# Output gates by seven block products for two pairs of chunks, in a bidirectional hybrid encoder layer

## The chip, the cores and the metric

The kernel runs on one core of a Trainium2 chip. The metric is the device time of one execution in microseconds. The kernel before takes 1054.59 us (median of 3 runs, 1054.48 to 1054.64).

## The reference, cut to what matters

One layer over 1024 tokens of width 1024, all in float32:

```python
h  = rmsnorm(x)
gb, gc, gv, q, k, v, go, lr_f, lr_b = split_cols(h @ w_in)    # go: 512 columns
y_a = gb * dwconv3(gc * gv, conv_a)
y_b = silu(go) * headnorm(gla(q, k, v, decay(lr_f)) + flipped gla(..., decay(lr_b)))   # 4 heads
x  = x + rmsnorm(concat(y_a, y_b) @ w_out)
h  = rmsnorm(x)
u  = dwconv3(h @ w_up)                                        # 2 x 2816 columns
x  = x + rmsnorm((silu(u_gate) * u_val) @ w_down)
```

The change is about `go`, the output gates: `h @ w_in[:, 2560:3072]`, then silu. Each head of the gated linear attention (gla) has 128 of these columns.

## The kernel before

**Arithmetic.** TensorE multiplies in a reduced float format, so each operand is split in a high and a low part: ACT casts the high part (`copy`), DVE subtracts it from the original (`tensor_sub`) and gets the low part, and a product takes three passes (high x high, high x low, low x high). A weight chunk of 128 columns by 1024 tokens, `feature_chunk` (matmuls at L257), is 8 blocks of the contraction x 3 passes x 2 halves of the tokens = 48 matmuls of 128x512. `load_cols` loads its weights (DMA at L224) and splits them (L215 on ACT, L216 on DVE).

**Stages, in the order of TensorE.** (1) Norm, transposes into `hT` (the high and low parts of h, transposed, in two halves of 512 tokens) and the projection for v and the two small decay inputs, one tile of 128 tokens after another. (2) Four output gate chunks, `swish_gate(h)`: 48 matmuls into a PSUM tile `pgo`, then silu on ACT into `yT[4 + h]` (L298). (3) Four heads, `gla_head(h)`, interleaved with 12 chunks of the short convolution (`conv_tile`, chunks `gc`, `gv`, `gb`). (4) The product with w_out and the second norm. (5) The up projection, whose products are made with block sums: a 2 x 2 block product in 7 products instead of 8, 12 matmuls each (`product`, called under L859). (6) The down projection, seven `big_product`s of 132 matmuls (L1190), which run in the order 2, 1, 3, 6, 5, 7, 4. (7) The last norm and the output.

**One head.** On TensorE: `pqk` (queries and keys, a feature chunk), `pg` (L513, log decay), `pko` (L547, transposes of the decayed keys `cum`), `kv` (L580, states), `sc` (L561, scores), `po` (L635 scores x values, L638 queries x states). Between them, in TensorE's queue, stand the matmuls of convolution chunks and of the next head's `pqk`. On the way from `pg` to `pko`: ACT Abs, Exp, Ln of `pg` into `cum`; DVE subtracts (L521), runs two scans (L522, L523), copies `cl` (L527, L528); ACT Exp; DVE multiplies queries and keys (L536, L534, L537) and ends with `cum` times keys (L538). From `kv` to L638: ACT copies the states from PSUM into `S` (L588, L592), DVE runs 28 dependent steps over `S` (L597, L601). In DVE's queue the operations of head h and of head h + 1 are mixed.

**Jobs on GpSimd (POOL).** The up and down projections need sums of blocks of their weights. A job loads two tiles of 512 KB, makes four 128x512 sums or differences (`block_sums` at L108 to L111, `down_end` at L146 to L149), and stores the tiles to DRAM. There are 17 jobs: wu0 to wu3 (w_up), wp4 and wp5 (w_up, chunks 4 and 5), q0 to q10 (w_down). `side()` takes the next job from the list; with `ahead=1` its loads are begun one job before its sums. Before the change `side` is called in token tiles 2 to 7, after each gate chunk and at the first head, so twelve jobs (wu0 to wu3, q0 to q7) are begun there; five follow in the w_out stage. `tc.issue_after(i)` holds an instruction behind another one of the same engine, in that engine's queue.

Of the kernel before, what the change touches and what calls it, by code (L numbers as in the profile page):

```python
# [40 lines left out]
def kernel(  # L41
# [114 lines left out]
    jobs = [(up_begin, up_end, i) for i in range(4)] + [(down_begin, down_end, q) for q in range(8)]  # L156
    jobs += [(pair_begin, pair_end, c) for c in (4, 5)] + [(down_begin, down_end, q) for q in range(8, NQ)]
# [136 lines left out]
    def swish_gate(h):
        w = load_cols([(w_in, O_GO + h * P, P)], f"go{h}")
        ps = feature_chunk(w, hT, f"pgo{h}")
        yT[4 + h] = ypool.tile([P, L], F32, tag="y", name=f"yT{4 + h}")
        nc.scalar.activation(yT[4 + h], ps, AF.Silu)  # L298

    act_table("natural_log_exp_and_others")  # L300
    with ExitStack() as n1:
# [195 lines left out]
    left = []  # L497

    def gla_head(h):

# [43 lines left out]
        def decayed():  # L544
# [4 lines left out]
            nc.scalar.copy(tiles["koT"], pk)  # L549
# [179 lines left out]

# [595 lines left out]
```

## Time and profile before

| | |
|---|---|
| median of the runs | 1054.59 us |
| the profiled execution, its own time | 1054.48 us |
| its span | 1052.8 us (1.7 us lie around it) |
| granted TensorE clock, mean | 0.998 |
| busy: PE, PEld, DVE, ACT, POOL | 1040.6, 871.0, 797.7, 466.5, 260.4 us |
| stage: token tiles | until 66 us |
| stage: gates | 66 to 111 us, then `pqk` of head 0 until 122 us |
| stage: four heads and the convolution | 122 to 321 us |
| stage: w_out | 321 to 436 us |
| stage: up | 436 to 836 us |
| stage: down | 836 to 1016 us, and the tail to 1052.8 us |

PE is TensorE's matmuls, PEld its weight loads (they run beside matmuls), DVE VectorE, ACT ScalarE, POOL GpSimd, SP the engine that issues most DMAs. In the timeline a line gives start, duration, engine, line of the program, operation, and out<-in; a bracket at the end gives the idle time of the engine before it and what ended that. `x2` groups two instructions of one kind.

### The profile page before, as it was taken

Reading aid. Unit: us, or ns where it says so; the run is one execution under the profiler, and the core shown is the slowest. Engines: PE = TensorE matmul, PEld = TensorE weight load, DVE = VectorE, ACT = ScalarE, POOL = GpSimd, SP = SyncE. Lnnn points to the kernel's source line nnn. Section 1 sums busy time; section 2 is a strip of 40 time slices with the busy share of each in tenths; the row PEclk is TensorE's granted clock in tenths of the full one; section 3 lists DMA queues with packets and bytes.
Section 4 is the critical chain, followed back from the end, with each engine's and each line's share of the span. In section 5 each row is a group of like instructions: output and inputs, shape, how many; then the busy total and the mean of one; then the engine's idle time right before and its main releaser. Section 6 shows DMA issues by size and latency. Waiting matters only on the chain.

```text
span 1052.8 us, 14126 instructions
## 1 busy us (share of the span) xinstructions
PE 1040.6 (99%) x5409; PEld 871.0 (83%) x5409; DVE 797.7 (76%) x991; ACT 466.5 (44%) x637; POOL 260.4 (25%) x253
## 2 busy tenths in 40 slices
PE   8999999999999999999999999999999999999997
PEld 7998888888888888887888888888888888888886
DVE  6843379889877877989977977987897875545566
ACT  5431353553434345644434344344443564344443
POOL 2797830000015810002242241241240000000011
PEclk9999999999999999999999999999999999999999
DMA  8888730110166853264323233332323687666555
GB/s 287 283 272 289 249 110 21 52 49 21 40 222 207 290 181 110 90 180 140 121 90 110 100 103 98 124 112 85 110 100 121 200 275 258 206 197 197 167 170 209
DMA packets 125701, 164.48 MB, mean 156 GB/s; under 512 B 16177, under 2 KB 83138, under 8 KB 125634
## 3 DMA queue, kind: packets, MB, share of 16 engines
q1 hardware_dynamic: 113762, 121.24, 36.3%
q0 software_dynamic: 11152, 40.38, 10.8%
q10 hardware_dynamic: 720, 1.97, 0.5%
q8 instruction: 42, 0.69, 0.3%
q14 instruction: 25, 0.20, 0.1%
HBM read 117.16 MB, written 46.40 MB: 155 GB/s over the span
## 4 chain that ended last, share of the span: by engine, by line
PE 94%; DVE 4%; DMA 1%; issue 0%; ACT 0%; SPq 0%; DVEq 0%; ACTq 0%
PE pb L859 16%; PE pc L859 11%; PE pdb L1190 10%; PE pa L859 10%; PE pw L785 8%; PE pgv L257 4%; PE pgc L257 4%; PE pqk L257 4%; PE pgo L257 4%; PE pv L368 4%; PE pgb L257 3%; PE pdd L1190 3%; PE pdc L1190 3%; PE pda L1190 3%; PE pdl L1190 1%; PE kv L580 1%
## 5 line engine op out<-in xcount | busy, mean ns | idle before, releaser
L1190 PE MATMUL pdb<-d 128*128 128x512 f32 (+1 forms) x495 | 109.5, 382 | 0.0
L1190 PEld LDWEIGHTS pdb<-d 128*128 128x128 f32 x495 | 90.8, 188 | 18.0
L859 PE MATMUL pb<-t,uv 128*128 128x512 f32 x264 | 63.4, 389 | 0.0
L1238 POOL DMA_DIRECT2D x2r<-x2d x4 | 2.2, 542 | 227.9 <-DMA d_8r<-actd 218.6
L859 PEld LDWEIGHTS pb<-t,uv 128*128 128x128 f32 x264 | 49.6, 188 | 10.3
L1073 DVE TENSOR_TENSOR cg<-cv,pb 128x512 f32<-128x512 f32 x22 | 15.1, 685 | 35.2 <-PE pb L859 17.7
L1121 ACT ACTIVATE uu<-uu 128x1024 f32<-128x1024 f32 x22 | 23.4, 1062 | 36.1 <-DVE uu L1043 35.9
L123 POOL COPY wp4g<-ident 128x1 f32<-128x1 f32 x1 | 0.2, 191 | 154.6 <-PE pgc L257 154.6
L1079 ACT COPY cg<-pa 128x512 f32<-128x512 f32 x22 | 12.9, 585 | 46.5 <-PE pa L859 46.5
L1042 DVE SCALAR_TENSOR_TENSOR uv<-cv,prm,uv 128x1023 f32<-128x1023 f32 x22 | 31.7, 1439 | 0.0
L1190 PE MATMUL pdc<-d 128*128 128x512 f32 x132 | 30.1, 389 | 0.0
L1190 PE MATMUL pdd<-d 128*128 128x512 f32 x132 | 30.1, 389 | 0.0
L1190 PEld LDWEIGHTS pdd<-d 128*128 128x128 f32 x132 | 24.8, 188 | 5.1
L1190 PEld LDWEIGHTS pdc<-d 128*128 128x128 f32 x132 | 24.8, 188 | 5.1
L1043 DVE SCALAR_TENSOR_TENSOR uu<-cg,prm,uu 128x1023 f32<-128x1023 f32 x22 | 28.9, 1314 | 0.0
L1043 DVE SCALAR_TENSOR_TENSOR uv<-cv,prm,uv 128x1023 f32<-128x1023 f32 x22 | 28.1, 1277 | 0.0
L1042 DVE SCALAR_TENSOR_TENSOR uu<-cg,prm,uu 128x1023 f32<-128x1023 f32 x22 | 28.1, 1276 | 0.0
L929 POOL TENSOR_TENSOR us61r<-uv6r 128x512 f32<-128x512 f32 x1 | 1.3, 1343 | 106.4 <-ACT us4bh L731 106.4
L1124 DVE TENSOR_TENSOR uu<-uu,uv 128x1024 f32<-128x1024 f32 x22 | 27.3, 1240 | 0.0
L597 DVE SCALAR_TENSOR_TENSOR S<-S,dec 64x128 f32<-64x128 f32 x56 | 19.2, 344 | 10.3 <-ACT S L588 8.5
L1041 ACT ACTIVATE uu<-cg,prm 128x1024 f32<-128x1024 f32 x22 | 25.2, 1144 | 2.9 <-ACT uv L1041 1.5
L1041 ACT ACTIVATE uv<-cv,prm 128x1024 f32<-128x1024 f32 x22 | 25.4, 1155 | 1.2 <-DVE cv L1101 0.6
(1204 smaller groups left out, 3170.0 us busy)
## 6 DMA issues: line engine op xcount, KB each, us to landing
actd<-as SPq DMA_DIRECT2D x20, 512.0 KB
x<-in_x_dram SPq DMA_DIRECT2D x16, 512.0 KB, 6.0
actd<-uu SPq DMA_DIRECT2D x10, 512.0 KB, 3.5
x2d<-x SPq DMA_DIRECT2D x8, 512.0 KB, 3.3
actd<-uu SPq DMA_DIRECT2D x10, 256.0 KB, 2.0
out_dram<-o POOLq DMA_DIRECT2D x5, 512.0 KB, 6.6
x2r<-x2d POOLq DMA_DIRECT2D x4, 512.0 KB, 3.7
x2r<-x2d SPq DMA_DIRECT2D x4, 512.0 KB, 3.6
```

The source lines that it names most:

```text
L257: nc.tensor.matmul(o[hf], wt[:, k, :], act[hf][a][:, k, :], start=(k == 0 and wt is wh and a == 0), stop=(k == KT - 1 and wt is wl))
L368: keep(nc.tensor.matmul(ps[:, n * 512 : n * 512 + VH], a[:, k, sl], w[:, k % 2, n * VH : (n + 1) * VH], start=(j == 0), stop=(j == 3 * KT ...
L597: nc.vector.scalar_tensor_tensor(S[0:DK, c + 1, :], S[0:DK, c, :], dec[0:DK, c : c + 1], S[0:DK, c + 1, :], op0=ALU.mult, op1=ALU.add)
L785: ins = nc.tensor.matmul(ps[:, n * HALF : (n + 1) * HALF], a[:, k, sl], w[:, n * HALF : (n + 1) * HALF], start=(i == 0 and q == 0), stop=( ...
L859: nc.tensor.matmul(o, w[:, k, :], m[:, k, :], start=start and k == 0 and q == 0, stop=k == 3 and q == 2, skip_group_check=True)
L1041: nc.scalar.activation(u, src, AF.Copy, scale=ffn_tap(1, r))
L1042: nc.vector.scalar_tensor_tensor(u[:, 1:L], src[:, 0 : L - 1], ffn_tap(0, r), u[:, 1:L], op0=ALU.mult, op1=ALU.add)
L1043: nc.vector.scalar_tensor_tensor(u[:, 0 : L - 1], src[:, 1:L], ffn_tap(2, r), u[:, 0 : L - 1], op0=ALU.mult, op1=ALU.add)
L1073: nc.vector.tensor_add(cg[:, hi], cv[:, lo], pb)
L1121: last_act[0] = nc.scalar.activation(ug, ug, AF.Silu)
L1124: nc.vector.tensor_mul(ug, ug, uv)
L1190: nc.tensor.matmul(o, a[:, 0, sl], b[:, 1, r], start=start and i == 0, stop=stop and i == 2, skip_group_check=True)
```

## The change

**Products.** The four gate chunks become two pairs (heads 0 and 1, heads 2 and 3). For a pair, the 1024 contraction rows are halved, the tokens are halved, and the two chunks are the two blocks of columns. Seven products of 12 matmuls replace eight: 84 matmuls for a pair, 168 in all instead of 192. Some operands are sums of blocks. Those of h (`gs`, `gl`, in token tiles 4 to 7, in `gate_sums`, `gate_sum_1`, `gate_sum_4`) are made by DVE and, for one of them, by POOL, and are then split into `gt1` to `gt4`. Those of the weights are made by POOL with `block_sums` on the raw weights `go0r`, `go1r` (second pair: `go2r`, `go3r`) and are then split into `gs02`, `gs03` (`gs12`, `gs13`) and `gv`. The raw weights of the second pair are loaded into the same buffers, so their loads stand behind DVE's split of the first pair. The results of products are added from PSUM by DVE into the gate rows `cg`, `cv`, which are `yT[4]` to `yT[7]`.

**Order on TensorE.** After the token tiles: two products that need no sums, the small transposes `pprm` and `plr`, two more such products, then `pqk` of head 0, whose result stays in its PSUM tile until head 0 takes it; then five products of pair 0 and five of pair 1; then `pg` of head 0. From `pg` on, TensorE's order is that of before.

**Silu.** The four silus move from behind each gate chunk to the first head: behind ACT's copy of `koT` of head 0, with a table load ahead and one behind. Abs of head 1 (`cum`) stands behind the last silu.

**Jobs.** Only wu0 is begun in the token tiles. wu1 to wu3 are begun when a late gate row is written (`cg[1]`), q0 at the first head, q1 and wp4 behind heads 0 and 1. wp5 and q2 to q6 come in the w_out stage, and q7 to q10 in the down stage, behind the first evict.

**Smaller moves.** The set-up of `mask`, `rst` and `Am` moves from the start to behind the gates, `up_raw` to the pool of the token tiles; some small buffers get other counts. In the last token tile's `finish`, two halves of 512 columns on DVE replace 512 and 256 columns on DVE and 256 on ACT and POOL.

The diff, cut to its core:

```diff
-    jobs = [(up_begin, up_end, i) for i in range(4)] + [(down_begin, down_end, q) for q in range(8)]
-    jobs += [(pair_begin, pair_end, c) for c in (4, 5)] + [(down_begin, down_end, q) for q in range(8, NQ)]
+    jobs = [(up_begin, up_end, i) for i in range(4)] + [(down_begin, down_end, q) for q in range(2)]
+    jobs += [(pair_begin, pair_end, c) for c in (4, 5)] + [(down_begin, down_end, q) for q in range(2, NQ)]
...
+    def gate_sums(i, ps):
...
+        nc.scalar.copy(last, ps[:, 4:8, :])
+        nc.vector.tensor_sub(t3, last, ps[:, 0:4, :])
+        nc.vector.tensor_add(t2, t3, hT[0][0][:, 0:4, sl].bitcast(F32))
+        nc.vector.tensor_add(t2, t2, hT[0][1][:, 0:4, sl].bitcast(F32))
...
+    def gate_sum_4(i):
...
+        nc.gpsimd.tensor_sub(t4, hT[0][0][:, 4:8, sl].bitcast(F32), t4)
+        nc.gpsimd.tensor_add(t4, t4, hT[0][1][:, 4:8, sl].bitcast(F32))
...
+    def gate_sums_w(rg, rv, w):
+
+        split(w[:, 0], w[:, 1], rv[:, 4:8])
+        block_sums(*(r.rearrange("p (a k) n -> p a (k n)", a=2) for r in (rg, rv)))
...
-            if t >= 2:
-                side(after=hs[t][:, 0:1], ahead=1)
-
-        swish_gate(0)
-        side(ahead=1)
+            if t == 2:
+                side(after=hs[t][:, 0:1])
...
+    ps_qk0 = feature_chunk(qk0, hT, "pqk0")
...
+    for p in range(2):
+        w = gs[p]
+        pb, pc = bank(f"pgb{p}"), bank(f"pgc{p}")
+        product(pb, w["s2"], gT[2], True)
+        nc.vector.tensor_add(cg[p][:, hi], cv[p][:, lo], pb)
+        product(pc, w["s1"], gT[1], True)
+        added = nc.vector.tensor_add(cv[p][:, hi], cv[p][:, lo], pc)
+        if p == 0:
+            rg, rv = gate_load(2), gate_load(3)
+            w1 = wpool.tile([P, 2, 4, P], F32R, tag="w", name="gv1")
+            with tc.issue_after(added.ins):
+                gs.append(gate_sums_w(rg, rv, w1))
+        product(pb, w["s3"], gT[3], False)
...
+        product(pc, w["s4"], gT[5], False)
+        nc.vector.tensor_add(cg[p][:, hi], cg[p][:, hi], pc)
+        product(pb, w["a22"], gT[4], False)
+        nc.vector.tensor_add(cv[p][:, lo], cv[p][:, lo], pb)
...
-    for h in range(1, HEADS):
-        swish_gate(h)
-        side(ahead=1)
-    act_table("natural_log_exp_and_others")
-    side(ahead=1)
+    for p in range(3):
+        side(after=cg[1][:, HALF : HALF + 1], ahead=1)
...
+        if h == 0:
+
+            with tc.issue_after(copied[0].ins):
+                for row in yT[4:]:
+                    gated[0] = nc.scalar.activation(row, row, AF.Silu)
+            act_table("natural_log_exp_and_others")
...
+        if h < 2:
+            side()
...
+    while jobs:
+        side(late_tile if len(jobs) % 3 == 0 else spare_tile, y[0][:, 0:1])
...
-        for r in (slice(0, D),) if whole else (lo, slice(HALF, 768)):
+        for r in (lo, hi) if t == NT - 1 else (slice(0, D),):
```

**What moves in the queues.** ACT, from the copy of `koT` of head 0 to the first copies of states into `S`, before:

```order
L549 COPY koT_1466<-pko_1457 128x1024
L508 COPY kd_1438<-pqk_1388 64x1024
L588 COPY S<-kv_0_1480 64x4x128
L592 COPY S<-kv_0_1480 64x3x128
L588 COPY S<-kv_0_1480 64x4x128
```

The same place in the changed kernel (`yT_1065` and `yT_908` are gate rows 4 and 5):

```order
L696 COPY koT_1483<-pko_1474 128x1024
L858 ACT_TABLE_LOAD
L858 ACTIVATE yT_1065<-yT_1065 128x1024
L654 COPY kd_1455<-pqk_1405 64x1024
L858 ACTIVATE yT_908<-yT_908 128x1024
L735 COPY S<-kv_0_1497 64x4x128
L739 COPY S<-kv_0_1497 64x3x128
L735 COPY S<-kv_0_1497 64x4x128
```

A table load and two silus now stand ahead of the copies of states; the two other silus and a second table load stand behind the last of these copies.

DVE, from the scores of head 0 (`A`) to the subtraction of head 1 (`m`), through the last steps of head 0 over `S`, before:

```order
L568 TENSOR_TENSOR A_1443<-Am 128x512
L601 SCALAR_TENSOR_TENSOR S<-S,dec_1296 64x128 x3
L671 TENSOR_TENSOR c_1379<-c_1379,pgv_1450 128x1024
L601 SCALAR_TENSOR_TENSOR S<-S,dec_1296 64x128
L518 TENSOR_SCALAR m_1608<-pg_1605,prm 128x1024
L674 SCALAR_TENSOR_TENSOR u_1601<-c_1379,prm,u_1601 128x1023
L216 TENSOR_TENSOR gc1l<-gc1r,gc1h 128x1024
L675 SCALAR_TENSOR_TENSOR u_1601<-c_1379,prm,u_1601 128x1023
L521 TENSOR_TENSOR m_1608<-m_1608,cum_1609 128x1024
```

The same place in the changed kernel:

```order
L715 TENSOR_TENSOR A_1460<-Am 128x512
L748 SCALAR_TENSOR_TENSOR S<-S,dec_1313 64x128
L818 TENSOR_TENSOR c_1396<-c_1396,pgv_1467 128x1024
L748 SCALAR_TENSOR_TENSOR S<-S,dec_1313 64x128
L219 TENSOR_TENSOR gc1l<-gc1r,gc1h 128x1024
L748 SCALAR_TENSOR_TENSOR S<-S,dec_1313 64x128
L821 SCALAR_TENSOR_TENSOR u_1618<-c_1396,prm,u_1618 128x1023
L748 SCALAR_TENSOR_TENSOR S<-S,dec_1313 64x128
L822 SCALAR_TENSOR_TENSOR u_1618<-c_1396,prm,u_1618 128x1023
L665 TENSOR_SCALAR m_1630<-pg_1627,prm 128x1024
L668 TENSOR_TENSOR m_1630<-m_1630,cum_1631 128x1024
```

`gc1l` and the first `u` now stand ahead of the last step over `S`. Further on, the product `cum` times keys of head 1, the last one before `pko` of head 1, before:

```order
L688 TENSOR_TENSOR yT_1636<-u_1601,pgb_1637 128x1024
L538 TENSOR_TENSOR cum_1609<-cum_1609,kd_1438 128x1024
L646 TENSOR_REDUCE ssh_1721<-on_1720 128x8
L216 TENSOR_TENSOR gv1l<-gv1r,gv1h 128x1024
L195 TENSOR_SCALAR rv<-ssh_1721,eps 128x8
```

and in the changed kernel:

```order
L684 TENSOR_TENSOR kin_1644<-kin_1644,kd_1455 128x1024
L219 TENSOR_TENSOR gv1l<-gv1r,gv1h 128x1024
L793 TENSOR_REDUCE ssh_1743<-on_1742 128x8
L685 TENSOR_TENSOR cum_1631<-cum_1631,kd_1455 128x1024
L198 TENSOR_SCALAR rv<-ssh_1743,eps 128x8
```

A low part of weights and a reduction now stand ahead of it.

POOL, the last job before the w_out stage (q7: tiles `wd14r`, `wd15r`) and the start of the next, before:

```order
L146 TENSOR_TENSOR wd14r<-wd14r 128x512
L147 TENSOR_TENSOR wd14r<-wd15r,wd14r 128x512
L148 TENSOR_TENSOR wd15r<-wd15r,wd14r 128x512
L151 DMA wdd_89<-wd14r 128x1024
L149 TENSOR_TENSOR wd15r<-wd15r 128x512
L151 DMA wdd_89<-wd15r 128x1024
L123 COPY wp4g<-ident 128x1
```

In the changed kernel, a piece of POOL's queue behind the gates (the end of wu3, and q0: `wd0r`, `wd1r`):

```order
L140 DMA wd1r<-in_w_down_dram 128x1024
L110 TENSOR_TENSOR wu3g<-wu3v,wu3g 128x512
L115 DMA wud<-wu3v 128x2x512
L111 TENSOR_TENSOR wu3g<-wu3g 128x512
L146 TENSOR_TENSOR wd0r<-wd0r 128x512
L116 DMA wud<-wu3g 128x2x512
L147 TENSOR_TENSOR wd0r<-wd1r,wd0r 128x512
L148 TENSOR_TENSOR wd1r<-wd1r,wd0r 128x512
L151 DMA wdd_82<-wd0r 128x1024
L149 TENSOR_TENSOR wd1r<-wd1r 128x512
L151 DMA wdd_82<-wd1r 128x1024
```

Six jobs (wu1, wu2, wu3, q0, q1, wp4) now stand in POOL's queue between the gates and the w_out stage; there POOL's queue was empty before, but for the end of q6 and q7.

More of the change, by code (lines that the diff above doesn't have):

```diff
@@ L290, with split @@
     lrT = gp.tile([96, L], F32R, tag="lrT", name="lrT")
+    up96 = gp.tile([96, HEADS, P], F32R, tag="up96", name="up96")
+    gates = ExitStack()
+    tp = gates.enter_context(tc.tile_pool(name="tp", bufs=1, side="right"))
     yT = [None] * KT
[L294 to L298, printed above, removed]
+    def split(hi, lo, src):
+        nc.scalar.copy(hi, src)
+        nc.vector.tensor_sub(lo, src, hi.bitcast(F32))
@@ new lines, in product, with bank @@
+    def product(o, a, b, start):
+        (ah, al), (bh, bl) = a, b
+        for k in range(4):
+            for q, (w, m) in enumerate(((ah, bh), (ah, bl), (al, bh))):
+                nc.tensor.matmul(o, w[:, k, :], m[:, k, :], start=start and k == 0 and q == 0, stop=k == 3 and q == 2,
+                                 skip_group_check=True)
+    def bank(name):
+        return ps_tile(name)[:, 0:HALF]
+    g_sums = [None] * 4
+    g_last = [None] * 2
+    def gate_sums(i, ps):
+        sl = slice(i * P, (i + 1) * P)
+        if i % 2 == 0:
+            g_last[i // 2] = row_tile(f"gl{i}").rearrange("p (i k t) -> p i k t", i=2, t=P)
+        last = g_last[i // 2][:, i % 2]
+        g_sums[i] = row_tile(f"gs{i}").rearrange("p (k t) -> p k t", t=P)
+        t3, t2 = g_sums[i][:, 0:4], g_sums[i][:, 4:8]
+        nc.scalar.copy(last, ps[:, 4:8, :])
+        nc.vector.tensor_sub(t3, last, ps[:, 0:4, :])
+        nc.vector.tensor_add(t2, t3, hT[0][0][:, 0:4, sl].bitcast(F32))
+        nc.vector.tensor_add(t2, t2, hT[0][1][:, 0:4, sl].bitcast(F32))
@@ new lines, in gate_load, with gate_operand, gate_weights @@
+    def gate_load(c):
+        raw = rawp.tile([P, KT, P], F32, tag="raw", name=f"go{c}r")
+        nc.sync.dma_start(out=raw, in_=w_in[:, :, O_GO + c * P : O_GO + (c + 1) * P])
+        return raw
+    def gate_operand(raw, shape, name):
+        h, l = (wpool.tile(shape, F32R, tag="w", name=f"{name}{x}") for x in "hl")
+        split(h, l, raw)
+        return h, l
+    def gate_weights(p, rg):
+        h, l = gate_operand(rg, [P, KT, P], f"go{p}")
+        return (h[:, 0:4], l[:, 0:4]), (h[:, 4:8], l[:, 4:8])
@@ new lines @@
+    tp2 = gates.enter_context(tc.tile_pool(name="tp2", bufs=3, side="right"))
+    for p in range(2):
+        product(pa[p], a[p][1], b1[1], False)
+    with tc.issue_after(copied.ins):
+        qk0 = load_cols([(w_in, O_Q, DK), (w_in, O_K, DK)], "qk0")
+    ps_qk0 = feature_chunk(qk0, hT, "pqk0")
+    w = rawp.tile([P, 2, 4, P], F32R, tag="raw", name="gv0")
+    t13, t24 = gate_tiles(0, ("3h", "3l")), gate_tiles(0, ("2h", "2l"))
+    gs = [gate_sums_w(rg, rv, w)]
+    gate_operands(gs[0], rg, rv, (t24, t13))
@@ L837 @@
         side(border_tile, ident[:, 0:1], ahead=1)
-    side()
-    assert not jobs and not begun
     h2_transpose(0)
@@ L842 @@
     w_out_tile(5)
+    side(border_tile, ident[:, 0:1])
     h2_transpose(2)
@@ L852, in w_tile @@
         return pool.tile(shape, F32R, tag="w", name=name)
-    def product(o, a, b, start):
-        (ah, al), (bh, bl) = a, b
-        for k in range(4):
-            for q, (w, m) in enumerate(((ah, bh), (ah, bl), (al, bh))):
-                nc.tensor.matmul(o, w[:, k, :], m[:, k, :], start=start and k == 0 and q == 0, stop=k == 3 and q == 2,
-                                 skip_group_check=True)
     def spare_tile(name):
```

114 lines of the change are left out of this document (81 added, 33 removed).

## Prediction

> **What bounds the kernel now.** First the page: busy times and the chain that ended last.
>
> ```profile
> PE 1040.6 (99%) x5409; PEld 871.0 (83%) x5409; DVE 797.7 (76%) x991; ACT 466.5 (44%) x637; POOL 260.4 (25%) x253
> PE 94%; DVE 4%; DMA 1%; issue 0%; ACT 0%; SPq 0%; DVEq 0%; ACTq 0%
> ```
>
> PE is busy for 99% of the span and carries 94% of the chain: a matmul removed is time gained, as long as its place isn't taken by a wait. So the second view is the busy time by stage, to see which engine stands closest behind PE (columns: length, then busy time of PE, PEld, DVE, ACT, POOL; granted clock; DMA share; GB/s).
>
> ```profile
> 22.00:66.00 44.00, 44.00 (x360) 44.00 (x358) 31.91 (x49) 18.68 (x37) 36.22 (x47) 1.00 0.81 268
> 66.00:122.00 56.00, 56.00 (x254) 46.24 (x253) 17.71 (x16) 11.88 (x14) 45.99 (x47) 1.00 0.85 277
> 122.00:321.00 199.00, 199.00 (x1432) 164.30 (x1431) 168.67 (x243) 98.08 (x125) 21.93 (x25) 1.00 0.27 85
> 836.00:1016.00 180.00, 180.00 (x796) 149.09 (x795) 101.62 (x97) 80.55 (x87) 2.17 (x4) 1.00 0.69 219
> 1016.00:1053.00 37.00, 30.26 (x165) 26.25 (x163) 27.26 (x64) 15.54 (x46) 5.83 (x7) 0.95 0.46 171
> ```
>
> In the gates (66 to 122) DVE has 17.71 us of work in 56, and POOL is full: its jobs lie where nobody needs DVE. In the heads (122 to 321) it is the reverse: DVE works 168.67 of 199 us and POOL 21.93. The change takes PE time from the first stage and puts POOL's jobs into the second. Third, the chain in order of time (start, duration) gives the deadlines that PE sets.
>
> ```profile
> 59.88 6.25 PE pv L368 x50
> 66.13 10.93 PE pgo L257 x48
> 111.03 10.88 PE pqk L257 x48
> 121.92 0.47 PE pg L513 x2
> 145.55 0.87 PE pko L547 x8
> 171.95 1.90 PE po L638 x32
> 186.32 0.87 PE pko L547 x8
> ```
>
> I call the start of `pg` T (121.92 here). PE reaches `pko` of head 0 at T + 23.6, the product of queries and states of head 0 (L638) at T + 50.0, and `pko` of head 1 at T + 64.4. PE's order behind `pg` doesn't change, so these distances hold if nothing waits.
>
> **Matmuls removed.** A chunk costs 10.93 us for 48 matmuls, 0.228 each; 24 go: 24 x 0.228 = 5.5 us less. That the work might not shrink isn't a case: 168 matmuls stand in the place of 192. T becomes 116.4.
>
> **The gates' own waits.** In the token tiles DVE gets about five 128x512 operations per tile (0.68 each by the first row here), 3.4 us in a period of 6.25. Four tiles add 13.7 to 31.91 of 44, but most of POOL's job sums leave this stage, and these lengthen DVE there (second row: minimum, median, maximum of `h` in ns).
>
> ```profile
> 1039.35 0.68 DVE L1292 TENSOR_TENSOR yg<-pdb,gpost 128x512 f32<-128x512 f32 x1
> L356 DVE SCALAR_TENSOR_TENSOR h<-x,rs,g x4: 1285/1818/2975, 29.6 to 50.1; 128x1024 f32<-128x1024 f32 x4
> 103.98 1.31 POOL L146 TENSOR_TENSOR wd8r<-wd8r 128x512 f32<-128x512 f32 x1
> wu2v<-in_w_up_dram POOLq DMA_DIRECT2D x1, 512.0 KB, 5.5
> go3r<-in_w_in_dram SPq DMA_DIRECT2D x1, 512.0 KB, 6.9
> wud<-wu2v POOLq DMA_DIRECT2D x1, 512.0 KB, 4.5
> ```
>
> I take 0 there (0 to 1.5). The `pqk` of head 0 between the first products and the rest covers 10.88 us of the preparing of pair 0: it delays nothing, being needed anyway. Pair 1 is tighter. Its raw weights are loaded into buffers that come free with DVE's low parts of pair 0, which PE needs at about 66.1 + 2 x 5.45 + 1.3 + 10.9 = 89.2. From about 88: a load of 5.5 to 6.9, four POOL sums of 1.3 (up to twice that beside DVE), a cast of 1.0 (ACT's `koT` below has that size) and a low part of 1.2 to 2.3 (DVE's `cum` times keys below, and beside a sum), so 101 to 107, and PE is there at 89.2 + 13.6 = 102.8. A wait of 0 to 4; I take 1.2, near the fast end, since DVE does little beside it. The set-up of `rst` and `mask` runs on POOL and DVE while ACT makes Abs, Exp and Ln, which hides it.
>
> **POOL's sums beside DVE, the term that decides.** Head 0 has the price, since the end of job q7 ran beside its chain. DVE there, then POOL, then the same DVE operations in head 1, where POOL rested:
>
> ```profile
> 130.15 3.26 DVE L522 TENSOR_TENSOR_SCAN cum<-rst,m 64x1024 f32<-64x1024 f32 x1
> 133.44 3.21 DVE L523 TENSOR_TENSOR_SCAN cum<-rst,m 64x1024 f32<-64x1024 f32 x1
> 136.68 1.09 DVE L527 COPY cl<-cum 64x16 f32<-64x16 f32 x1
> 138.00 2.66 DVE L536 TENSOR_TENSOR qd<-qd,m 128x1024 f32<-128x1024 f32 x1
> 143.99 1.21 DVE L538 TENSOR_TENSOR cum<-cum,kd 128x1024 f32<-128x1024 f32 x1
> 129.61 1.65 POOL L146 TENSOR_TENSOR wd14r<-wd14r 128x512 f32<-128x512 f32 x1
> 138.26 1.31 POOL L149 TENSOR_TENSOR wd15r<-wd15r 128x512 f32<-128x512 f32 x1
> 172.42 2.28 DVE L522 TENSOR_TENSOR_SCAN cum<-rst,m 64x1024 f32<-64x1024 f32 x1
> 174.74 2.29 DVE L523 TENSOR_TENSOR_SCAN cum<-rst,m 64x1024 f32<-64x1024 f32 x1
> 177.06 0.17 DVE L527 COPY cl<-cum 64x16 f32<-64x16 f32 x1
> 178.21 1.23 DVE L536 TENSOR_TENSOR qd<-qd,m 128x1024 f32<-128x1024 f32 x1 [0.78 <-ACT m L532]
> 182.76 1.22 DVE L538 TENSOR_TENSOR cum<-cum,kd 128x1024 f32<-128x1024 f32 x1
> ```
>
> 3.26 + 3.21 + 1.09 + 2.66 = 10.22 against 2.28 + 2.29 + 0.17 + 1.23 = 5.97: the four sums of that job (first and last shown) cost DVE 4.25, 1.06 each. [...]
>
> When do the jobs run? wu1 is begun when a late gate row is written, 2 us ahead of T, and its second load stands on POOL's queue behind the set-up of `rst`, so it lands near T + 7.6. From then on a job is a load (5.5), four sums (2.1 each beside DVE) and a store (4.5), and each later load waits for the store of an earlier job, since the buffers go round: wu1's sums from T + 8 to 17, wu2's from 22 to 29, wu3's from 30 to 41, q0's from 41 to 50, q1's from 57 on.
>
> - `pko` of head 0. Its chain ends at 143.99 + 1.21 = 145.20, 0.35 ahead of PE, with four sums beside it. wu1 brings four again, perhaps one of wu2, and the chain starts a little earlier, as queries and keys are there already. 0.3, from 0 to 2.
> - The two silus ahead of `S`. The rows of ACT:
>
> ```profile
> 77.71 1.28 ACT L298 ACT_TABLE_LOAD   x1
> 79.00 1.03 ACT L298 ACTIVATE yT<-pgo 128x1024 f32<-128x1024 f32 x1
> 146.80 1.01 ACT L549 COPY koT<-pko 128x1024 f32<-128x1024 f32 x1
> 148.06 1.01 ACT L508 COPY kd<-pqk 64x1024 f32<-64x1024 f32 x1 [0.25 <-DVE kd L507]
> 150.33 0.58 ACT L588 COPY S<-kv 64x512 f32<-64x512 f32 x1 [1.25 <-PE kv L580]
> 152.01 2.62 DVE L597 SCALAR_TENSOR_TENSOR S<-S,dec 64x128 f32<-64x128 f32 x7 [3.99 <-ACT S L588]
> 166.06 0.35 DVE L601 SCALAR_TENSOR_TENSOR S<-S,dec 64x128 f32<-64x128 f32 x1
> ```
>
>   A load of 1.28 and two silus of 1.03 make 3.34, and ACT idles 0.25 + 1.25 = 1.50 there: the states start 1.8 later, at T + 31.9. The steps ended at 166.41, T + 44.5; with 1.8 more and `gc1l` and `u` ahead of the last one (2.4) at T + 48.7, still 1.3 ahead of L638. No wait yet, but of the former 5.5 us of room 1.3 are left.
> - `pko` of head 1. Its chain ended at 182.76 + 1.22 = 183.98, 2.34 ahead of PE. 1.8 later, and behind a low part and a reduction (1.1 each by their spacing), less 0.8 of a DVE wait that they fill: 1.8 + 2.2 - 0.8 = 3.2, so PE waits 0.9.
> - The sums beside this stretch. From T + 32 to T + 65 DVE was busy almost without a gap, and only some 5 of 33 us are operations that read PSUM, which I let run free. Of wu3 three sums fall in it, of q0 four, of q1 up to four. I count seven: q1 comes last and behind two landings more. 7 x 1.06 x 28/33 = 6.3 before `pko` of head 1; about 4 of them already at L638. Bounds: 0, if the jobs slip into DVE's idle time, and 11 x 1.06 x 28/33 = 9.9.
>
> **Behind the heads.** The third and fourth silu and the second table load stand behind the copies of `S`, where ACT had 4 us free. The w_out stage keeps its six jobs. In the down stage four jobs bring 8 loads and 8 stores of 0.52 MB, 8.4 MB, beside a DMA share of 0.69 at 219 GB/s, and 16 sums; DVE has 101.62 of 180 us of work there, and the first product that needs them is the fourth of seven (big product 6), some 90 us after the stage's start. 0, up to 4. The tail:
>
> ```profile
> 1048.09 1.61 DVE L1259 SCALAR_TENSOR_TENSOR o<-yg,rs,x2r 128x512 f32<-128x512 f32 x2
> ```
>
> 512 and 256 columns took 1.61 with POOL beside them; two halves alone are 2 x 0.68 = 1.36, with a larger last store behind. 0, within 0.3 either way.
>
> **The sum**, against the profiled execution's own 1054.48 (0.1 below the median): -5.5 + 1.2 + 0.3 + 0.9 + 6.3 = +3.2, so 1057.7. The 5.5 us that PE saves come back, and more, as waits of PE on DVE at L638 of head 0 and `pko` of head 1.
>
> **Rivals.**
> 1. *The sums miss DVE's tight stretch* (faster). If job landings slip, wu3 and q0 fall into the idle time ahead of the steps over `S` and behind `pko` of head 1, or steps of 0.35 us slip between POOL's operations. For it: DVE idles 3.99 us ahead of the first step, and a landing took 5.5 to 6.9 in a quieter or busier stage. Against: 28 of 33 us are SBUF work. Then the waits are 1.2 + 0.9, or less: -5.5 + 2.1 = -3.4, so 1051.1. It decides from three sums or fewer in the stretch.
> 2. *All of it*: eleven sums (9.9), and pair 1 of the gates late by 3. -5.5 + 3 + 0.3 + 0.9 + 9.9 = +8.6, so 1063.1.
> 3. *The clock falls behind a long wait.* In the last window of the table PE is busy for 30.26 of 37 us and the granted clock is 0.95, 1.9 us of 37; elsewhere PE hardly idles and it is 1.00. A wait of 4 us or more at L638 and another at `pko` would add 2 x 1.9: +7.0, so 1061.5. [...]
> 4. *The late jobs*: q7 to q10 reach the fourth big product late, by up to 4 us on top of the forecast: 1061.7.
>
> **How the numbers follow.** Chances: the forecast 0.42 (own range 1054 to 1061), rival 1 0.36, rival 2 0.12, rivals 3 and 4 0.05 each. A difference of 0.2%, 2.1 us, is about what a measurement of this kernel can tell from no change. Rival 1 lies below 1052.5 but for some 0.03; the forecast reaches into the 2.1 us on either side of no change with 0.08. So faster 0.33, the same 0.11, slower 0.56. The range leaves a tenth out at each end: from 1050.5, rival 1 with the gates' waits at nearly nothing, to 1063.5, rival 2.
>
> **What would show it.** Right: in the changed kernel's waits of PE, `po` <- DVE `S` (L638's place) with 3 to 6 us and `pko` of head 1 with another few; the steps over `S` taking longer than the 14.4 us from 152.01 to 166.41 by one us for each POOL sum beside them; PE's busy time 5.5 us lower. Wrong: PE waits of under 3 us in all between `pg` and the end of head 1, or sums of wu3 and q0 outside T + 32 to T + 65; a PE wait in the gates above 4 us; a wait of `pdb` on operands in the down stage.

## The result: 16.3 us slower

The changed kernel takes 1070.91 us (median of 4 runs, 1069.62 to 1071.28) against 1054.62 us for the kernel before in the same session (4 runs, 1054.48 to 1054.83): a ratio of 1.0152, interval 1.0135 to 1.0170. The profiled execution took 1070.88 us with a span of 1069.1 us, so its span is 16.3 us longer than the 1052.8 us of before.

The page of the changed kernel, busy times, granted clock over the span and the chain that ended last:

```profile
PE 1042.1 (97%) x5385; PEld 871.2 (81%) x5385; DVE 844.9 (79%) x1037; ACT 480.0 (45%) x664; POOL 295.6 (28%) x274
PEclk9999997899999999999999999999999999999999
PE 87%; DVE 8%; ACT 2%; DMA 1%; issue 1%; POOL 0%; SPq 0%; DVEq 0%; POOLq 0%; ACTq 0%
```

There are 24 matmuls fewer, but PE's busy time did not fall; it rose by 1.5 us. The clock line tells why: in the seventh and eighth slice, a fortieth of the span each, the clock was at 7 and 8 tenths, and matmuls took longer there (12 in 4.58 us below). And DVE now carries 8% of the chain instead of 4%. The stages of gates, heads and down, in the table of windows (length, then PE, PEld, DVE, ACT, POOL; clock; DMA share; GB/s):

```profile
66.00:118.26 52.26, 50.97 (x228) 41.31 (x226) 27.89 (x39) 18.39 (x28) 15.39 (x14) 1.00 0.28 71
118.26:337.70 219.44, 205.60 (x1433) 169.65 (x1432) 185.44 (x243) 104.42 (x130) 70.31 (x76) 0.95 0.38 123
850.00:1030.00 180.00, 180.00 (x795) 149.03 (x795) 110.59 (x98) 81.04 (x89) 37.94 (x43) 1.00 0.80 268
```

The down stage is as full of matmuls as before. All of the damage is in the heads, where PE is idle for 219.44 - 205.60 = 13.8 us, with a clock of 0.95, and POOL has gone from about 22 us of work to 70. The waits of PE there and in the gates (total, times, longest):

```profile
PE po L785 <- DVE S L748: 5.5, 1, 5.5
PE po L782 <- DVE A L715: 5.2, 1, 5.2
PE pko L694 <- DVE rv L198: 3.2, 1, 3.2
PE pgb L311 <- ACT gs12h L303: 0.8, 1, 0.8
PE pgb L311 <- DVE gs12l L304: 0.5, 1, 0.5
```

Three waits on DVE, 13.9 us in all, in head 0 and at `pko` of head 1. To see which of them sets the end, I take four marks of PE, all from the timeline (the chain gives starts that differ by up to 0.2 us): the start of `pg` of head 0 (T), of `pko` of head 1, of the first product with w_out (`pw`), and the end of the span. The last two marks of the changed kernel, then those of before:

```profile
200.22 1.94 PE L694 MATMUL pko<-ident,cum 128*128 128x128 f32 x8 [3.17 <-DVE rv L198]
337.74 0.62 PE L933 MATMUL pw<-wo4h,yh 128*128 128x512 f32 x2
```

```profile
121.75 0.63 PE L513 MATMUL pg<-lrT,up 96*128 96x512 f32 x2
186.16 1.04 PE L547 MATMUL pko<-ident,cum 128*128 128x128 f32 x8
321.17 0.61 PE L785 MATMUL pw<-wo4h,yh 128*128 128x512 f32 x2
```

| stretch | before | after | difference |
|---|---|---|---|
| start to T | 121.75 | 118.26 | -3.5 |
| T to `pko` of head 1 | 64.41 | 81.96 | +17.55 |
| `pko` of head 1 to `pw` | 135.01 | 137.52 | +2.5 |
| `pw` to the end of the span | 731.6 | 731.4 | -0.2 |

The four differences make 16.35 us, the whole result. In the second stretch the chain of the changed kernel leaves PE altogether. Its first long piece and its last one on DVE there, and what follows:

```profile
150.89 1.98 DVE S L744
...
198.94 1.13 DVE cum L685
...
202.16 4.58 PE pgc L260 x12
```

Between the first step over `S` and `cum` times keys of head 1, 48 us, the chain runs along DVE. The last line shows the lowered clock: 12 matmuls in 4.58 us, where 0.228 each would be 2.7. What DVE did in those 48 us, beside POOL's operations in the same stretch:

```profile
150.51 11.35 DVE L744 SCALAR_TENSOR_TENSOR S<-S,dec 64x128 f32<-64x128 f32 x7 [5.97 <-ACT S L735]
161.90 1.81 DVE L748 SCALAR_TENSOR_TENSOR S<-S,dec 64x128 f32<-64x128 f32 x1
179.67 0.35 DVE L748 SCALAR_TENSOR_TENSOR S<-S,dec 64x128 f32<-64x128 f32 x1
188.53 1.09 DVE L674 COPY cl<-cum 64x16 f32<-64x16 f32 x1
198.86 1.21 DVE L685 TENSOR_TENSOR cum<-cum,kd 128x1024 f32<-128x1024 f32 x1
```

```profile
151.41 1.29 POOL L109 TENSOR_TENSOR wu3v<-wu3g,wu3v 128x512 f32<-128x512 f32 x1
162.25 1.30 POOL L149 TENSOR_TENSOR wd1r<-wd1r 128x512 f32<-128x512 f32 x1
170.32 1.26 POOL L146 TENSOR_TENSOR wd2r<-wd2r 128x512 f32<-128x512 f32 x1 [2.19 <-DMA wd2r<-in_w_down_dram]
176.50 1.67 POOL L149 TENSOR_TENSOR wd3r<-wd3r 128x512 f32<-128x512 f32 x1
187.70 1.90 POOL L108 TENSOR_TENSOR wp4v<-wp4v 128x512 f32<-128x512 f32 x1 [2.46 <-DMA wp4v<-in_w_up_dram]
193.90 1.70 POOL L111 TENSOR_TENSOR wp4g<-wp4g 128x512 f32<-128x512 f32 x1
```

Seven steps that took 2.62 us before take 11.35, and the copy `cl` 1.09 instead of 0.17. Fifteen sums lie beside the stretch from 150.51 to 198.86 + 1.21 = 200.07: three of wu3 (from 151.41), four of q0 (to 163.55), four of q1 (170.32 to 178.2) and four of wp4 (187.70 to 195.6). The forecast had counted seven.

### The profile page after: what moved, and what is told of

The parts are those of the page before. It is cut to its first block, busy times and chain, and to the rows that moved or that the text cites. A ratio compares the mean times of both kernels' runs of the same rounds, so it can differ in the third digit from the quotient of the medians.

```text
span 1069.1 us, 14218 instructions
## 1 busy us (share of the span) xinstructions
PE 1042.1 (97%) x5385; PEld 871.2 (81%) x5385; DVE 844.9 (79%) x1037; ACT 480.0 (45%) x664; POOL 295.6 (28%) x274
## 4 chain that ended last, share of the span: by engine, by line
PE 87%; DVE 8%; ACT 2%; DMA 1%; issue 1%; POOL 0%; SPq 0%; DVEq 0%; POOLq 0%; ACTq 0%
PE pb L311 16%; PE pc L311 11%; PE pdb L1325 10%; PE pa L311 9%; PE pw L933 8%; PE pgc L260 4%; PE pv L453 4%; PE pgv L260 3%; PE pqk L260 3%; PE pdd L1325 3%; PE pdc L1325 3%; PE pda L1325 3%; PE pgb L260 2%; DVE S L744 1%; PE pdl L1325 1%; PE pga L311 1%
## 5 line engine op out<-in xcount | busy, mean ns | idle before, releaser
L1208 DVE TENSOR_TENSOR cg<-cv,pb 128x512 f32<-128x512 f32 x22 | 15.0, 684 | 35.3 <-PE pb L311 18.1
L1256 ACT ACTIVATE uu<-uu 128x1024 f32<-128x1024 f32 x22 | 23.4, 1062 | 35.9 <-DVE uu L1178 35.9
L744 DVE SCALAR_TENSOR_TENSOR S<-S,dec 64x128 f32<-64x128 f32 x56 | 28.0, 500 | 12.2 <-ACT S L735 10.5
L946 ACT ACTIVATE tmp<-x 128x1024 f32<-128x1024 f32 x8 | 8.5, 1061 | 44.0 <-DVE x L943 44.0
```

Of the source, the lines that this page charges most:

```text
L744: nc.vector.scalar_tensor_tensor(S[0:DK, c + 1, :], S[0:DK, c, :], dec[0:DK, c : c + 1], S[0:DK, c + 1, :], op0=ALU.mult, op1=ALU.add)
L1208: nc.vector.tensor_add(cg[:, hi], cv[:, lo], pb)
L1256: last_act[0] = nc.scalar.activation(ug, ug, AF.Silu)
```

## The experiments

Theory: the sums that now lie beside DVE's tight stretch hold DVE up, each by about 1.06 us, and nothing else of the change costs much. Rivals: the two silus and the table load ahead of the states; the low clock behind PE's waits; the block products themselves; the jobs' transfers. For each experiment I give the distance from T to `pko` of head 1 (64.41 before, 81.96 after) and from there to `pw` (135.01, 137.52), read as above. Where no interval stands, the time is one run.

### The sums alone

```diff
-        block_sums(ag, av)
+        if k == 0:
+            block_sums(ag, av)
...
-        block_sums(ag, av)
+        if c != 4:
+            block_sums(ag, av)
...
+        if q >= 2:
+            nc.gpsimd.tensor_sub(w1[:, lo], w1[:, hi], w1[:, lo])
...
```

> The changed kernel without the 24 sums on POOL of the six jobs that stand between the gates and the w_out stage (wu1 to wu3, q0, q1, wp4); their loads and stores stay, so what they store is the raw weights and the output is not the reference's. Theory 1 (POOL's sums beside DVE's steps over S make PE wait, and the clock falls behind these waits): the steps over S fall from 29.5 us to about 17 us, PE waits at L782 and L785 of head 0 go (10.7 us), the one at pko of head 1 (3.2) falls below 1.5, the granted clock stays 1.00 in the heads, and the time is 1050 to 1053 us. Rival (two silus ahead of S, and the new order on DVE, do it): the waits stay above 8 us and the time above 1063 us. Rival (the jobs' transfers disturb): the same, above 1063 us.

Measured: 1052.18 us, 2.4 below the kernel before. The distances are 66.28 and 134.82. PE waits 1.7 us at `pko` of head 1. Its DVE:

```profile
150.09 2.62 DVE L747 SCALAR_TENSOR_TENSOR S<-S,dec 64x128 f32<-64x128 f32 x7 [5.97 <-ACT S L738]
152.98 0.35 DVE L751 SCALAR_TENSOR_TENSOR S<-S,dec 64x128 f32<-64x128 f32 x1 [0.26 <-ACT S L742]
166.69 0.35 DVE L751 SCALAR_TENSOR_TENSOR S<-S,dec 64x128 f32<-64x128 f32 x1
182.76 1.22 DVE L688 TENSOR_TENSOR cum<-cum,kd 128x1024 f32<-128x1024 f32 x1
```

The seven steps are back at 2.62 us and both waits at `po` are gone, though every job's loads and stores still run. So in the heads the transfers cost nothing that shows, and neither do the block products. The stretch takes 182.76 + 1.22 - 150.09 = 33.89 us here and 49.56 in the changed kernel: 15.67 us for 15 sums, 1.04 each. Of the distance to `pko`, 81.96 - 66.28 = 15.7 of the 17.55 us are the sums; the other 1.9 are the silus and the order of DVE.

### Half of the sums

```diff
-        block_sums(ag, av)
+        if c != 4:
+            block_sums(ag, av)
...
+        if q >= 2:
+            nc.gpsimd.tensor_sub(w1[:, lo], w1[:, hi], w1[:, lo])
...
```

> The changed kernel without the 12 sums of q0, q1 and wp4, whose loads and stores stay; wu1 to wu3 keep their sums, so the output is not the reference's. A dose between e1 (no sums, 1052.2) and the changed kernel (1070.9). Theory 1: three or four sums of wu3 are left beside the steps over S of head 0; the waits of PE at L785 and pko of head 1 are 4 to 6 us together, each under 3, and the time is 1055 to 1058 us. If the three jobs' transfers or ACT's silus mattered beside the sums: above 1060 us.

Measured: 1057.43 us; the distances are 70.6 and 134.82. Its seven steps, with the three sums of wu3 beside them:

```profile
150.16 7.16 DVE L746 SCALAR_TENSOR_TENSOR S<-S,dec 64x128 f32<-64x128 f32 x7 [5.97 <-ACT S L737]
```

With the sums of q0, q1 and wp4 left out the time falls by 13.5 us, with those of wu1 to wu3 as well by 5.2 more. Position decides: q0, q1 and wp4 have all of their 12 sums in the stretch and cost 11.4 us of the distance to `pko` (81.96 - 70.6); wu1 to wu3, with three of 12 in it, cost 4.3 (70.6 - 66.28). These three are dearer than the mean: the seven steps take 7.16 - 2.62 = 4.5 us more, 1.5 for each sum.

### The jobs without the block products

The kernel before, with only the list of jobs and the places of `side` as in the changed kernel:

```diff
-    jobs = [(up_begin, up_end, i) for i in range(4)] + [(down_begin, down_end, q) for q in range(8)]
+    jobs = [(up_begin, up_end, i) for i in range(4)] + [(down_begin, down_end, q) for q in range(2)]
...
     next(gla[0])
+    for p in range(3):
+        side(after=first_qd[0][:, 0:1], ahead=1)
     next(gla[0])
     side()
...
+        if h < 2:
+            side()
...
```

> The kernel before with its jobs alone moved to the places of the changed kernel: wu0 in the token tiles, wu1 to wu3 behind the queries of head 0, q0 at the first head, q1 and wp4 behind heads 0 and 1, q7 to q10 in the down stage; four chunks of gates, silus and DVE's order as before. Theory 1 (POOL's sums): PE waits at L635 or L638 of head 0 and at pko of head 1, 6 to 12 us together, the clock falls behind them, and the time is 1062 to 1072 us. Rival (block products, silus and DVE's order do it): within 2 us of 1054.6.

Measured: 1076.36 us, 21.9 above the kernel before and more than expected; the distances are 81.49 and 137.50. Its waits of PE:

```profile
PE po L639 <- DVE A L572: 5.3, 1, 5.3
PE pko L551 <- DVE cum L542: 5.2, 1, 5.2
PE po L642 <- DVE S L605: 4.1, 1, 4.1
```

The same three waits at the same three places, with no block product and no moved silu in the program. So the move of the jobs makes the loss in the heads by itself, 17.1 + 2.5 us; another 2.2 lie behind `pw` (733.8 us to the end of the span). The whole change is 5.5 us faster than this: 3.5 of it ahead of T (121.78 against 118.26) and 2.4 behind `pw`, less 0.5 that it loses between.

### The silus

No silu of the gates and no table load in head 0:

```diff
-            with tc.issue_after(copied[0].ins):
-                for row in yT[4:]:
-                    gated[0] = nc.scalar.activation(row, row, AF.Silu)
-            act_table("natural_log_exp_and_others")
+            gated[0] = copied[0]
```

> The changed kernel without the four silus and the two table loads in the first head, so the gates go in without silu and the output is not the reference's. Theory 1 (POOL's sums): the steps over S start some 2 us earlier, and the waits of PE shrink by 2 to 3 us of 13.9; the time is 1067 to 1069.5 us. Rival (silus ahead of S): the waits at L782, L785 and pko of head 1 go for the most part and the time is below 1058 us.

All four silus behind the copies of `S`:

```diff
-            with tc.issue_after(copied[0].ins):
+            with tc.issue_after(last_act[0].ins):
```

> The changed kernel with all four silus and the table load behind the last copy of states of head 0, in place of two ahead of these copies. Theory 1 (POOL's sums): copies of S and the steps start about 2 us earlier, the waits fall by about as much; 1067.5 to 1069.5 us. Rival (silus ahead of S): below 1060 us.

Measured: 1067.3 us without silus, 1067.86 with all of them behind. The distances to `pko` are 78.17 and 78.40, in both cases 3.6 to 3.8 less than in the changed kernel. With the sums in place, where the silus stand is worth 3.0 us of the time, and the half microsecond between these two runs is less than the spread of the changed kernel's own four runs (1069.62 to 1071.28). It is a part of the loss, but by far the smaller one: 1067 is still 13 us above the kernel before.

### Sums that read nothing

To see whether it is POOL's being busy or what it reads, each sum is replaced by a fill of a whole tile, which only writes and takes 0.97 us:

```diff
+    def fills(*tiles):
+        for w in tiles:
+            for i in range(2):
+                nc.gpsimd.memset(w, float(i))
...
```

> The changed kernel with each of the 24 sums of the six jobs in the heads replaced by one memset of 128x1024 on POOL, which writes about as long (0.94 us against 1.3) but reads nothing; loads and stores stay, and the output is not the reference's. If what DVE and POOL share is the reading of SBUF, the steps over S run as without sums (about 17 us) and the time is 1051 to 1054 us. If any use of SBUF by POOL blocks DVE, each memset costs about 0.8 us and the time is above 1060 us.

Measured: 1056.74 us, between the two cases; the distances are 67.58 and 137.58. Four of POOL's fills, then DVE:

```profile
150.95 0.95 POOL L116 MEMSET wd0r<- 128x1024 f32 x1
...
176.33 0.97 POOL L116 MEMSET wp4g<- 128x1024 f32 x1
179.00 1.96 POOL L116 MEMSET wp4v<- 128x1024 f32 x2 [0.66 <-DMA wp4v<-in_w_up_dram]
```

```profile
150.43 2.62 DVE L758 SCALAR_TENSOR_TENSOR S<-S,dec 64x128 f32<-64x128 f32 x7 [5.99 <-ACT S L749]
175.88 1.46 DVE L688 COPY cl<-cum 64x16 f32<-64x16 f32 x1
179.85 1.22 DVE L695 TENSOR_TENSOR cum<-cl,cum 128x1024 f32<-128x1024 f32 x1
```

The fill at 150.95 lies beside the seven steps, and these take 2.62 us as if POOL rested; the two from 179.00 to 180.96 don't lengthen the product of 1.22 beside them either. One operation is held, the small copy `cl`: it ends at 177.34, when the fill from 176.33 ends, after 1.46 us instead of 0.17. These 1.3 us are the whole difference between this distance and that without sums (67.58 - 66.28). So in this kernel the seven steps, DVE operations on SBUF alone, were held by POOL's sums, which read and write (11.35 us), and not by its fills, which only write (2.62), and in one case a copy was held by a fill. How a step and a sum share their time shows at the start of the steps in the changed kernel: the sum from 151.41 keeps its 1.29 us and ends at 152.70, and the step over `S` beside it, whose row begins at 150.89, ends at 152.87, behind the whole sum.

Of the rest against the run without sums, 137.58 - 134.82 = 2.8 us lie behind `pko` of head 1, where the clock is lower. That is the next point.

### The clock

PE's clock in the changed kernel, in windows of 4 us:

```profile
172.00:176.00 4.00, 1.99 (x32) 1.61 (x32) 3.87 (x5) 1.88 (x2) 3.36 (x4) 0.50 0.22 66
180.00:184.00 4.00, 3.92 (x33) 3.59 (x34) 3.83 (x5) 0.00 (x0) 0.41 (x1) 0.50 0.81 248
200.00:204.00 4.00, 3.78 (x13) 3.42 (x14) 3.76 (x9) 3.40 (x4) 0.00 (x0) 0.50 0.35 105
```

Behind each of the three waits the clock is at 0.50. To see what that costs, 22 matmuls of 128x512 with results that nobody uses are put ahead of the product of scores and values in head 0, so that PE has work while it waits for `A`:

```diff
+        if h == 0:
+            for _ in range(22):
+                nc.tensor.matmul(po[:, 0:HALF], hT[0][0][:, 0, 0:P], hT[0][0][:, 0, :], start=True, stop=True)
```

> The kernel of e10_warm once more: 22 matmuls of 128x512 more on PE ahead of L782 of head 0, 5.0 us of work in a wait of 5.2. If the granted clock falls because PE rests: L782 runs in 1.0 us again in place of 2.0; PE then rests until S is ready (6.4 us), and what follows is as slow as before; the time stays at 1069.5 to 1071.5 us. If the clock falls for another reason, L782 still takes about 2 us.

Measured: 1069.72 us, 1.2 less than the changed kernel's median though there is more work, but still within the range of its four runs. (A first run of this kernel gave 2713.66 us, on a chip where the kernel before also ran once at 3738.42 us; it is left out.) The rows of PE:

```profile
170.82 6.80 PE L777 MATMUL po<-hTh 128*128 128x512 f32 x22 [3.65 <-DVE Am L711]
177.55 1.10 PE L785 MATMUL po<-V,A 64*64 64x128 f32 x32
180.19 1.97 PE L788 MATMUL po<-S,qd 128*64 128x128 f32 x32 [1.53 <-DVE S L748]
```

The products of head 0 with `A` and with `S` run at full rate here, 1.10 and 1.97 us; in the changed kernel they took 1.99 and 3.68. A rest of 3.65 us is left ahead of the added matmuls, and the clock is lower behind it (0.73 from 172 to 176 us): the 22 take 6.80 us where 0.228 each would be 5.0. By their end the clock is back (1.00 from 176 to 180 us), and it stays at 1.00 behind the rest of 1.53 us (180 to 184). So with PE's rests of 5.2 and 5.5 us the clock is at 0.50 in head 0, and with the first cut to 3.65 and the second to 1.53 it is back at 1.00 by 176 us: it followed PE's rest. But `pko` of head 1 comes only 0.8 us earlier after T (81.16), because DVE sets that time and a slow PE had merely filled the waiting. What the clock costs is what lies behind `pko` of head 1: 12 matmuls took 4.58 us in the chain of the changed kernel. The same 12 in the chain without sums, where the wait was 1.7 us and the clock stayed at 1.00:

```profile
185.19 2.75 PE pgc L263 x12
```

With the slower `pko` itself (1.94 us against 1.06) this makes 2.7 us, as much as the third stretch is longer here than without sums (137.52 - 134.82); against the kernel before it is the 2.5 of the table. That stretch is 134.82 in both runs with sums left out, and 137.1 to 137.6 in every run above where `pko` took 1.94 us. Behind waits at `pko` of 1.0 us (half of the sums) and 1.7 us (no sums) the clock stayed at 1.00; behind one of 3.0 us (fills) it was at 0.60 and then 0.55, behind 3.2 us (changed kernel) at 0.50. The runs below show no fixed limit between these: a wait of 2.2 us was followed by a lower clock (0.83 from 140 to 150 us), and two waits of 2.6 us were not.

### Looking for another home for the jobs

q0, q1 and wp4 into the w_out stage, in tiles of the weights' ring:

```diff
-    side()
+    side(more=False)
...
-        if h < 2:
-            side()
...
+    side(border_tile, ident[:, 0:1], ahead=1)
     w_out_tile(5)
```

> The changed kernel with three of the six jobs taken out of the heads: q0, q1 and wp4 go to the w_out stage, which makes nine jobs there; wu1 to wu3 stay as they are. Theory 1 (POOL's sums): three sums of wu3 are left beside the steps over S, at 1.1 to 1.3 us each, so the waits of PE fall from 13.9 to 2 to 5 us, and the time is 1053 to 1057 us. Rival (moved sums are paid for elsewhere, in the w_out stage): the heads gain as much, but the w_out stage gets longer by over 3 us.

Measured: 1078.75 us, a miss; the loss in the w_out stage that its rival named came. The heads did what was expected: the distances are 69.65 and 134.81, with waits of 2.4 and 2.6 us, and `pko` of head 1 behind the second takes 1.07 us, where it took 1.94 at the low clock. But behind `pw` the span has 754.8 us left, 23.4 more than in the changed kernel. Of these, 16.0 are one wait of PE in the w_out stage, and the first matmuls behind it are slow: eight transposes `tx` take 1.97 us, where sixteen take 1.91 in the changed kernel. That wait, and ACT's operation ahead of it:

```profile
PE tx L959 <- DVE b1l L304: 16.0, 1, 16.0
```

```profile
395.68 1.04 ACT L303 CAST ug0h<-ug0r 128x1024 fp32r<-128x1024 f32 x1 [21.00 <-POOL wd10r L147]
```

ACT stood for 21 us at a cast of up weights; the profile puts the end of that down to POOL's sum `wd10r` of a job, and the casts that the transposes `tx` need were queued behind it. The result of that cast and the tiles of the jobs take their buffers from one pool (`wpool`); that the cast waited for such a buffer is likely, but was not tested. Two more runs add to this, both far above what was expected of them: wu3's sums held until `cum` times keys of head 1 is done, without and with the silus behind.

```diff
+        if h == 1:
+            held = gp.tile([P, 1], F32, tag="held", name="held")
+            with tc.issue_after(nc.gpsimd.tensor_copy(held, cum[:, 0:1]).ins):
+                side(more=False)
```

> As e6_moved, and the sums of wu3 held until the last product of the decayed keys of head 1, in DVE's idle time ahead of the steps over S of head 1. Theory 1: no sum lies beside the steps over S of head 0 any more; what is left is the wait of 1 to 2 us at pko of head 1 that silus and DVE's order make; 1051.5 to 1053 us.

> As e7_held, and all four silus behind the copies of states of head 0, which also gives DVE the order of the kernel before around the steps over S. Theory 1: no wait of PE in the heads; the heads last 199.4 us as before, and of the 5.45 us of removed matmuls all but the 1.5 to 2 us of waits in the gates are gained; 1050.5 to 1051.5 us, 0.3% faster than before.

Measured: 1078.85 us (ratio 1.0232, interval 1.0217 to 1.0247) and 1079.95 us (1.0253, 1.0234 to 1.0271); the wait in the w_out stage is back in both, with 18.1 and 16.0 us. In the heads, `pko` of head 1 stands at 66.30 and 64.39 after T: with no sum beside the stretch and the silus behind, the distance of before is back to within 0.02 us, and the place of the silus is worth 1.9 us, just what the run without sums had left over. But the held sums then meet the small operations of the head's norm. From the second run:

```profile
185.85 1.73 DVE L206 TENSOR_TENSOR rs<-rs,rt 128x8 f32<-128x8 f32 x1
```

An operation of 0.17 us takes 1.73, two ahead of it 1.25 and 1.26, PE waits 2.6 us ahead of the transposes `pot` behind them, with the clock staying at 1.00 (from 184 to 196 us), and the way from `pko` to `pw` grows by 4.0 us (139.01).

Last, the jobs spread further, with the silus behind: only wu1 and wu2 in the heads, six in the w_out stage, four in the up stage.

```diff
-    for p in range(3):
+    for p in range(2):
...
+        if c in (5, 9, 13, 17):
+            side(spare_tile)
```

> The changed kernel with its jobs spread anew, nothing left out: in the heads only wu1 and wu2, whose sums fall beside the chain of head 0 (where q7 ran before) and into DVE's idle time ahead of S; wu3, wp4, wp5, q0, q1, q2 in the w_out stage (six jobs, as in the changed kernel), q3 to q6 in the up stage behind chunks 5, 9, 13 and 17, q7 to q10 in the down stage; all four silus behind the copies of states of head 0. Theory 1 (POOL's sums beside the heads were the loss): no wait of PE over 1 us in the heads, they last 199.4 us as before, the gates keep waits of 1.5 to 2 us, and the time is 1050.5 to 1052 us. Rival (the sums are paid for wherever they stand): the up stage gets longer by 2 us or more, 1053 us and above.

Measured: 1100.03 us (1.0434, 1.0418 to 1.0451), the worst. Its waits of PE, the longest of four that ACT has for a transfer in the up stage, and the window around `pko` of head 0:

```profile
PE pc L311 <- DVE cv L1220: 19.3, 5, 5.8
PE pko L694 <- DVE cum L685: 2.2, 1, 2.2
```

```profile
ACT us19ah L303 <- DMA wdd<-wd12r: 11.0, 1, 11.0
```

```profile
140.00:150.00 10.00, 7.77 (x36) 5.90 (x36) 7.58 (x4) 5.00 (x5) 5.91 (x5) 0.83 0.75 228
```

From `pw` to the down stage this run needs 560.5 us instead of 514.8. In the up stage four casts of weights on ACT wait for 9.5 to 11.0 us each until the store of a job's tile has landed; the results of these casts and the jobs' tiles come from the same pools (`w_tile`). DVE is busy there for 333 of 402 us, so that it is full is not shown. So this run and the three before it say little about the price of sums in those stages, since the jobs held buffers there that casts needed, here by the waits shown and in the other three likely. In the heads even wu1 and wu2 alone cost 4.0 us: wu2's sums came earlier and met the chain to `pko` of head 0, and that wait of 2.2 us lowered the clock (0.83 from 140 to 150 us).

No version that does the whole work beat the kernel before. 1052.18 us, with 24 sums left out, is an estimate of what this change would give if the sums cost nothing where they stand.

## Why the prediction was wrong

The direction and the mechanism were right, the size was not: 1057.7 was forecast, with a range to 1063.5. Its steps, one by one:

| term | forecast | measured | from |
|---|---|---|---|
| 24 matmuls and the gates' waits | -5.5 + 1.2 = -4.3 | -3.5 | T |
| `pko` of head 0 | +0.3 | 0 | no wait there |
| silus and the order of DVE | +0.9 | +1.9 | distance without sums |
| sums beside DVE's stretch | +6.3 | +15.7 | distance with and without sums |
| clock | 0 (rival: 3.8) | +2.5 | third stretch |
| late jobs, tail | 0 | -0.2 | last stretch |

Ahead of T, the waits on `gs12h` and `gs12l` are 1.3 us, as forecast; if the matmuls gave their 5.5, another 0.7 is lost there. Most of it lies at the same two waits: from 100.05 to T stand 72 matmuls, 16.4 us at 0.228 each, and they take 18.2, which is 1.8 lost in place of 1.3.

**The step that failed** is the count: "I count seven: q1 comes last and behind two landings more". Fifteen sums lay there. At the forecast's own 1.06 x 28/33 = 0.90 each, fifteen would have made 13.5 us of the measured 15.7. Two errors made the count. First, a sum was taken as 2.1 us beside DVE; beside the short steps it kept its 1.3, so q0 ran from T + 38.8 to T + 45.3 instead of T + 41 to 50, and q1 began at T + 52. Second, the stretch was held at its old length. It ended at T + 65 only if no sum held it up; each sum that does moves the end by about a microsecond and gives the next job time to arrive. So the steps over `S` lasted until T + 61.8, q1 met them with all of its sums, and wp4, which the forecast didn't count in any case, met the rest. Even the upper bound of eleven sums, 9.9, stopped at the old end of the stretch.

**The price** was right as a mean only, 1.04 us against 1.06, and that was luck. Against the run without sums, the seven sums of wu3 and q0 cost (161.90 + 1.81 - 150.51) - (152.98 + 0.35 - 150.09) = 9.96 us, 1.42 each, more than a sum lasts. The four of q1 cost 2.6, 0.65 each, and the four of wp4 3.1, 0.78 each. That operations which read PSUM run free, the 28/33 of the term, was the author's assumption, read from no row of before. It was right where a sum met one: `c`, which adds from the PSUM tile `pgv`, takes 1.22 us with a sum beside it, and 1.22 in the run without sums.

```profile
172.87 1.22 DVE L818 TENSOR_TENSOR c<-c,pgv 128x1024 f32<-128x1024 f32 x1
173.34 1.28 POOL L147 TENSOR_TENSOR wd2r<-wd3r,wd2r 128x512 f32<-128x512 f32 x1
```

The short steps made up for it. The price of a sum hangs on what stands beside it.

**The clock** (rival 3) was given 0.05 as a rival, on top of the forecast, with 2 x 1.9. It came in with the waits it was tied to; that it depended on them should have made it a part of each case with a wait of that length. No row of before shows the 4 us in it; in the changed kernel the clock was at 0.50 behind waits of 5.2, 5.5 and 3.2 us. Its first fall, behind the two waits at `po`, cost little, as the run with the added matmuls shows; the second cost 2.5.

**Rival 1**, that the sums miss the stretch, didn't happen; its time, 1051.1, is close to that of the run without sums, 1052.18. **Rival 2** had the right idea and too few sums. **Rival 4** fell: the down stage is busy for 180.00 of 180 us and no time is lost behind `pw`. Of the marks that were to tell right from wrong, the waits at `po` for `S` and at `pko` of head 1 came, and one of 5.2 us for `A` that the forecast didn't name; PE's busy time rose by 1.5 us instead of falling by 5.5, since the clock was low; the steps over `S` took 179.67 + 0.35 - 150.51 = 29.5 us, against 16.95 without sums: 12.6 for the eleven beside them, 1.14 each. Two slips in its working change nothing: the latest end of pair 1's preparing adds up to 108.6, not 107, and the w_out stage had five jobs before, not six.

## What to carry to other kernels

An idle GpSimd is no free place: its sums over SBUF cost a busy VectorE here about a microsecond each, from 0.65 to 1.4 by what stood beside them, the most beside short operations. Their place is a stage where VectorE has time to spare and where their tiles hold no buffer that another engine waits for, and the price belongs into the sum when they are moved. When work is put beside a chain that is already nearly late, count what it meets on the lengthened chain, not on the old one, and let the count run until it closes. And when a change frees 5 us on the engine that bounds, look first at what had to be moved out of that stage to make room.

## What the runs showed of the hardware that was not expected

- POOL's sums did not get longer beside DVE steps of 0.35 us (1.28 to 1.31 us); the DVE side bore the loss there, and one step took 1.98 us beside a sum. In other places both lost: the sums of wp4, beside operations of 1.2 us and more, took up to 2.29 us, and DVE's `cum<-cl,cum` beside one of them 2.31 us instead of the 1.22 without sums.
- Fills by POOL, which read nothing, left the steps over `S` alone (2.62 us for seven) and one still held a DVE copy of 64x16 for 1.3 us, in the one case seen.
- Behind a PE wait of 2.2 us the clock was lower in one run (0.83 from 140 to 150 us); behind one of 2.6 us it was not in two others (1.00 in the one, `pko` in 1.07 us in the other). In head 0 the lowered clock cost little while DVE set the next deadline: 22 added matmuls that kept it up between the waits moved `pko` of head 1 by 0.8 us.
